# The last two expert loads in 16 transfers of 8 partitions each

## The chip, the cores and the metric

The kernel runs on one core of a Trainium2 chip. The metric is the time of one execution on the device in microseconds (us). TensorE (PE, with its weight loads as PEld), VectorE (DVE), ScalarE (ACT), GpSimd (POOL) and SyncE (SP) run side by side and wait for each other through semaphores. SP computes nothing here: it issues the transfers from the device's memory (HBM) to the on-chip memory of 128 partitions (SBUF). Sixteen DMA engines carry them.

## The reference

Two layers of an encoder on 256 tokens of width 1024, in float32, each sub-layer followed by a residual and a layer norm. Layer 0 mixes by retention and has a dense SwiGLU; layer 1 mixes by stick-breaking attention and has a mixture of experts. The change touches the experts alone:

```python
def moe_swiglu(x, w_router, w_in, w_out):
    ...
    top_val, top_idx = lax.top_k(logits, TOP_K)          # 2 of 8 experts for each token
    ...
    for e in range(N_EXPERTS):
        y = y + gates[:, e:e + 1] * swiglu(xt, w_in[e], w_out[e])
```

Here `swiglu(x, w_in, w_out)` is `(silu(x @ gate) * (x @ up)) @ w_out`, with 3584 hidden columns. The weights of one expert are 7168 x 1024 for `w_in` and 3584 x 1024 for `w_out`, 44 MB in all, and the eight experts' 352 MB are read once.

## The kernel before

The first part (retention, dense channel mixer, attention, router) fills about the first 520 us. In the second, the experts come one after the other, in an order that the router found at run time. SP reads an expert's number from a register, so each of its loads is preceded by an address calculation. Each expert is worked in two units of hidden columns, 2048 and 1536 (`UNITS`). For a unit TensorE multiplies the gathered tokens (in three blocks of 32) with the gate and the up columns (tile `pe`, line 1176), ScalarE and VectorE form `hs` and its transpose `hT`, and TensorE multiplies that with the unit's rows of `w_out` into `po`, also at line 1176.

The weights come in loads of 128 partitions, mostly 1 MB, into tiles called `raw`. A `Stream` keeps the list of them in the order of use. `pump` issues the next one as soon as one of the tiles is free, and a tile is freed (`used`) when its last part has been multiplied. All are issued by SP at line 217, in `chunk`. `by_row_plain` lists the loads of `w_out`: 256 rows each, where partition p takes the rows 2p and 2p + 1, 8 KB that lie together. So the last unit, of 1536 rows, has six; they will be called load 9 to load 14 here, with the eight of the unit before as load 1 to load 8. Each DMA on SP's queue has one of eight semaphores in turn (DMAHW0 to DMAHW7 in the program's rows), and waits, before it is issued, until the DMA that had the same one eight issues earlier has landed.

Behind load 14 SP issues four loads `gbt` of 256 KB (line 1330), the scale and offset of the last layer norm. At the end, TensorE adds up the residual (`psc`, line 1304), multiplies loads 9 to 12 and then loads 13 and 14 into `po`, and runs a few products `warm` (line 434) that nobody reads. `po` is copied to `y` (line 1236), and TensorE returns its rows to their tokens (`psc`, line 1316). The norm's statistics, `ot` (lines 1348 and 1351, then 1370 to 1375) and four stores (line 1366) follow. `by_need` takes the loads in groups of four row blocks at a time from `down`, which is why loads 9 to 12 form one group of eight row blocks and loads 13 and 14 the last.

A second pass of the experts (`more`) is in the program for the case that over 96 tokens choose one expert. It is not run with these inputs.

Of the kernel before, what the change touches and what calls it, by code (L numbers as in the profile page):

```python
# [23 lines left out]
P = 128  # L24
# [16 lines left out]
WARM = (6, 2, 1, 6)  # L41
RAW_MID = 6
RAW_END = 3
HL_BASE = 4
HL_EXTRA = 4

# [137 lines left out]
def trunk_kernel(ctx, tc, x, ret_w_in, ret_w_out, sb_w_kv, sb_w_q, sb_w_out, ln_mix_g, ln_mix_b,  # L184
                 ln_ffn_g, ln_ffn_b, ffn_w_in, ffn_w_out, moe_w_router, moe_w_in, moe_w_out,
                 const_a, const_r, out):
    nc = tc.nc
    ctx.enter_context(tc.manual_schedule())
    consts = ctx.enter_context(tc.tile_pool(name="consts", bufs=1))
    raws = ctx.enter_context(tc.tile_pool(name="raws", bufs=RAW_BASE))  # L190
    hls = ctx.enter_context(tc.tile_pool(name="hls", bufs=HL_BASE))
    res = ctx.enter_context(tc.tile_pool(name="res", bufs=1))
# [5 lines left out]
    def nm(s):  # L198
        cnt[0] += 1
        return f"{s}{cnt[0]}"  # L200
# [3 lines left out]


    def chunk(s, shape, src, cuts, pieces=1, after=None, between=None, plain=False,
              rows="(k p) f -> p k f"):

        def load(slots):
            r = slots.pool.tile([P, CH], F32, tag=slots.tag, name=nm("raw"))[:, :shape[0] * shape[1]]  # L210
            v = r.rearrange("p (k f) -> p k f", k=shape[0])
            for i, c in enumerate(cuts if pieces == 2 else [lambda v: v]):
                if i == 1 and between is not None:
                    between()
                for at, ap in src:
                    ap = ap() if callable(ap) else ap
                    nc.sync.dma_start(c(v[at]), c(ap.rearrange(rows, p=P)))
            if after is not None:
                after()
            return v  # L220
        s.add(load, cuts, plain)

    every = slice(None)

    def by_k(s, parts, after=None, between=None, **kw):

        cuts = [lambda v, i=i: v[:, 2 * i:2 * i + 2, :] for i in range(2)]
        for i in range(2):
            src, o = [], 0
            for ap, c0, n in parts:  # L230
                src.append(((every, every, slice(o, o + n)), ap[i * 512:(i + 1) * 512, c0:c0 + n]))
                o += n
            chunk(s, (4, 512), src, cuts, after=after and (lambda i=i: after(i)),
                  between=between and (lambda i=i: between(i)), **kw)

    def by_block(s, parts, **kw):

        src, o = [], 0
        for ap, c0, n in parts:
            src.append(((every, every, slice(o, o + n)), ap[:, c0:c0 + n]))  # L240
            o += n
        chunk(s, (8, 256), src, [lambda v, i=i: v[:, :, i * P:(i + 1) * P] for i in range(2)], **kw)

    def by_row(s, ap, r0, n, **kw):

        for r in range(r0, r0 + n, 256):
            chunk(s, (2, D), [((every, every, every), ap[r:r + 256, :])],
                  [lambda v, i=i: v[:, i:i + 1, :] for i in range(2)], **kw)

    def by_k_plain(s, ap, c0, n):  # L250

        for k in range(KD):
            chunk(s, (1, n), [((every, every, every), lambda k=k: ap()[k * P:(k + 1) * P, c0:c0 + n])],
                  [lambda v: v[:, 0, :]], plain=True)

    def by_row_plain(s, ap, r0, n):

        for r in range(r0, r0 + n, 256):
            chunk(s, (2, D), [((every, every, every), lambda r=r: ap()[r:r + 256, :])],
                  [lambda v, i=i: v[:, i, :] for i in range(2)], plain=True, rows="(p k) f -> p k f")  # L260

    def split(slots, v):

# [7 lines left out]

    base = Slots(hls, HL_BASE, "w")
    st = Stream([Slots(raws, RAW_BASE)], [base], split)
# [78 lines left out]
    def add_experts(s, which=None):  # L352

        prev = None
        for e in range(NE):
            dyn = e > 0 and which is not None

            def of(w, e=e, dyn=dyn):
                return w[ds(which[e], 1)].rearrange("o a f -> (o a) f") if dyn else w[e]

            for c0, n in UNITS:
                for o in (0, DE):
                    by_k_plain(s, lambda of=of: of(mw_in), o + c0, n)
                if prev is not None:
                    by_row_plain(s, *prev)
                prev = (lambda of=of: of(mw_out), c0, n)
        by_row_plain(s, *prev)

    which = [None] * NE
    add_experts(st, which)  # L370


# [230 lines left out]
    ap = att.enter_context(tc.tile_pool(name="attc", bufs=1, side="right"))  # L603
# [8 lines left out]
    i = (n_ffn - 8) % 8  # L612
# [162 lines left out]
    with tc.tile_pool(name="ffn", bufs=2, side="right") as fp, tc.tile_pool(name="ffn1", bufs=1, side="right") as fp1:  # L775
# [9 lines left out]
        def new_h():  # L785
            return [fp.tile([P, 4, S], FR, tag=tag, name=nm(tag)) for tag in ("hh", "hl")]
# [6 lines left out]
        for j in range(1, 6):  # L793
            old, hs = hs, fp.tile([P, 2, 512], F32, tag="hs", name=nm("hs"))
            if j > 1:
                prev, ht = ht, new_h()
# [12 lines left out]
            if j == 1:  # L809
                for t in range(2):  # L810
                    split_T(old[:, t, :256], *ht, t)
                prev, ht = ht, new_h()
# [56 lines left out]
    with att:  # L869
# [104 lines left out]
        mp2 = ctx.enter_context(tc.tile_pool(name="moe2", bufs=1, side="right", reuse_waits="tile"))  # L974
        raw_end = ctx.enter_context(tc.tile_pool(name="raw_end", bufs=RAW_END, side="right", reuse_waits="tile"))
        st.raws.append(Slots(raw_end, RAW_END))
        st.pump()
# [357 lines left out]
    def more(pos):  # L1335
        st2 = Stream([Slots(raws, RAW_BASE)], [base], split)
        add_experts(st2)
        st2.pump()
        g = one_hot(0, pos)
        experts(st2, pos, gates, g, gather(g), norm)  # L1340
# [62 lines left out]
```

## Time and profile before

| | |
|---|---|
| median of 3 runs | 1369.8 us (1368.88 to 1372.61) |
| the profiled execution | 1371.01 us, span 1369.2 us |
| TensorE busy | 1325.5 us, 97% of the span |
| mean granted TensorE clock | 0.997 |
| read from HBM | 444.08 MB, 325 GB/s over the span |
| DMA rate while the experts run | about 418 GB/s |

[...] Times in the rows count from the first instruction of the span. A busy TensorE is not TensorE at its peak, since matmuls overlap; whether it waits is seen from the idle time in brackets and what ended it. For DMA, the share says how many of the 16 engines are at work, and the time to landing counts from SP's issue to the last arrival.

### The profile page before, as it was taken

Reading aid. Unit: us, or ns where it says so; the run is one execution under the profiler, and the core shown is the slowest. Engines: PE = TensorE matmul, PEld = TensorE weight load, DVE = VectorE, ACT = ScalarE, POOL = GpSimd, SP = SyncE. Lnnn points to the kernel's source line nnn. Section 1 sums busy time; section 2 is a strip of 40 time slices with the busy share of each in tenths; the row PEclk is TensorE's granted clock in tenths of the full one; section 3 lists DMA queues with packets and bytes.
Section 4 is the critical chain, followed back from the end, with each engine's and each line's share of the span. In section 5 each row is a group of like instructions: output and inputs, shape, how many; then the busy total and the mean of one; then the engine's idle time right before and its main releaser. Section 6 shows DMA issues by size and latency. Waiting matters only on the chain. (4 is left out here: it accounts for less than half of the span.)

```text
span 1369.2 us, 30767 instructions
## 1 busy us (share of the span) xinstructions
PE 1325.5 (97%) x13611; PEld 865.6 (63%) x13611; DVE 446.5 (33%) x652; ACT 314.8 (23%) x465; POOL 46.7 (3%) x73
## 2 busy tenths in 40 slices
PE   9999999999999999999989999999999999999986
PEld 7888889999989884354434454563644563554543
DVE  6746667555565554101201200201200200210213
ACT  6544435444437642000100100100100100100101
POOL 0212101000010000000000000000000000000000
PEclk9999999999999999999999999999999999999999
DMA  9865437555649357999999999999999999999993
GB/s 336 295 213 179 160 97 272 179 190 185 185 127 357 131 183 295 393 418 417 418 418 418 416 420 418 417 418 419 400 418 420 406 418 420 401 417 419 405 415 155
DMA packets 122918, 447.40 MB, mean 327 GB/s; under 512 B 9088, under 2 KB 56976, under 8 KB 92048
## 3 DMA queue, kind: packets, MB, share of 16 engines
q1 hardware_dynamic: 121808, 442.01, 82.8%
q0 software_dynamic: 960, 3.15, 0.7%
q8 instruction: 123, 2.02, 0.6%
q14 instruction: 27, 0.22, 0.0%
HBM read 444.08 MB, written 1.05 MB: 325 GB/s over the span
## 5 line engine op out<-in xcount | busy, mean ns | idle before, releaser
L1176 PE MATMUL pe<-raw,xg 128*32 128x384 f32 (+1 forms) x5248 | 506.3, 540 | 13.4 <-PEq L1195 7.4
L1176 PEld LDWEIGHTS pe<-raw,xg 128*32 128x32 f32 x5248 | 203.9, 110 | 305.4 <-issue 266.6
L1176 PE MATMUL po<-raw,hT 128*32 128x256 f32 x4544 | 254.4, 379 | 8.4 <-DMA raw<-in_moe_w_out_dram 5.4
L269 DVE TENSOR_TENSOR w<-raw,w 128x1024 fp32r<-128x1024 f32 x162 | 198.1, 1234 | 144.5 <-ACT w L268 142.2
L1176 PEld LDWEIGHTS po<-raw,hT 128*32 128x32 f32 x4544 | 170.0, 110 | 95.6 <-issue 10.7
L268 ACT CAST w<-raw 128x1024 fp32r<-128x1024 f32 x162 | 168.4, 1048 | 134.6 <-issue 32.1
L1288 DVE TENSOR_TENSOR hs<-hs,pe 128x512 f32<-128x512 f32 (+1 forms) x48 | 29.1, 620 | 362.9 <-PE pe L1176 361.2
L1266 ACT ACTIVATE hs<-pe 128x512 f32<-128x512 f32 (+1 forms) x48 | 25.3, 544 | 457.7 <-PE pe L1176 457.7
L404 PE MATMUL pf<-xT_h,w 128*128 128x256 f32 x448 | 126.9, 283 | 0.0
L406 PE MATMUL pf<-xT_l,w 128*128 128x256 f32 x448 | 126.2, 282 | 0.0
L405 PE MATMUL pf<-xT_h,w 128*128 128x256 f32 x448 | 126.1, 281 | 0.0
L1290 DVE STREAM_TRANSPOSE hT<-hs 128x512 f32<-128x512 f32 (+1 forms) x48 | 27.2, 617 | 237.6 <-PE po L1176 139.2
L404 PEld LDWEIGHTS pf<-xT_h,w 128*128 128x128 f32 x448 | 84.4, 188 | 0.3
L405 PEld LDWEIGHTS pf<-xT_h,w 128*128 128x128 f32 x448 | 84.4, 188 | 0.3
L406 PEld LDWEIGHTS pf<-xT_l,w 128*128 128x128 f32 x448 | 84.4, 188 | 0.0
L1236 ACT COPY y<-po 32x256 f32<-32x256 f32 x48 | 17.5, 364 | 283.3 <-PE po L1176 238.7
L379 PE MATMUL pv<-w,xT_l 128*128 128x512 f32 x96 | 38.4, 400 | 0.0
L381 PE MATMUL pv<-w,xT_h 128*128 128x512 f32 x96 | 38.0, 396 | 0.3 <-DVE w L269 0.3
L380 PE MATMUL pv<-w,xT_h 128*128 128x512 f32 x96 | 37.9, 395 | 0.0
L404 PE MATMUL pq<-xT_h,w 128*128 128x256 f32 x128 | 36.3, 283 | 0.0
L406 PE MATMUL pq<-xT_l,w 128*128 128x256 f32 x128 | 36.0, 281 | 0.0
L405 PE MATMUL pq<-xT_h,w 128*128 128x256 f32 x128 | 36.0, 281 | 0.0
(237 smaller groups left out, 1180.5 us busy)
## 6 DMA issues: line engine op xcount, KB each, us to landing
raw<-in_moe_w_in_dram SPq DMA_DIRECT2D x128, 1024.0 KB, 19.9
raw<-in_moe_w_out_dram SPq DMA_DIRECT2D x112, 1024.0 KB, 19.8
raw<-in_moe_w_in_dram SPq DMA_DIRECT2D x128, 768.0 KB, 15.8
raw<-in_ret_w_in_dram SPq DMA_DIRECT2D x22, 1024.0 KB, 9.3
raw<-in_ffn_w_in_dram SPq DMA_DIRECT2D x20, 1024.0 KB, 5.1
raw<-in_ffn_w_out_dram SPq DMA_DIRECT2D x11, 1024.0 KB, 5.0
raw<-in_ret_w_out_dram SPq DMA_DIRECT2D x8, 1024.0 KB, 5.0
raw<-in_sb_w_kv_dram SPq DMA_DIRECT2D x4, 1024.0 KB, 6.0
```

The lines of the kernel that those rows point to most:

```text
L268: nc.scalar.copy(hv, v)
L269: nc.vector.tensor_sub(lv, v, hv.bitcast(F32))
L379: nc.tensor.matmul(o, sl, mh, start=first, stop=False)
L380: nc.tensor.matmul(o, sh, mh, start=False, stop=False)
L381: nc.tensor.matmul(o, sh, ml, start=False, stop=last)
L404: nc.tensor.matmul(o, lo[:, k, :], xT_h[:, k, :], start=(k == 0), stop=False)
L405: nc.tensor.matmul(o, h[:, k, :], xT_h[:, k, :], start=False, stop=False)
L406: nc.tensor.matmul(o, h[:, k, :], xT_l[:, k, :], start=False, stop=(k == KD - 1))
L1176: nc.tensor.matmul(ov, lhs[r], w, start=first and not (shared and r == 1), stop=last, skip_group_check=True)
L1266: nc.scalar.activation(pairs(hs[:, r, :]), alternate(pg[r]), AF.Silu)
L1288: nc.vector.tensor_mul(pairs(hs[:, r, :]), pairs(hs[:, r, :]), alternate(pu[r]))
L1290: nc.vector.transpose(hT[:, r].rearrange("p k s -> p (k s)"), hs[:, r, :])
```

## The change

`by_row_plain` gets a count of loads, `pieces`, that are cut up. For these, `chunk` issues one DMA for each eight partitions, 16 of 64 KB for one `raw` tile, in place of one DMA of 128 partitions. It is used for the last two loads of the last expert (`LAST8 = 2`): loads 13 and 14, 32 DMAs in place of two. Line numbers behind it grow by four.

```diff
+LAST8 = 2
...
     def chunk(s, shape, src, cuts, pieces=1, after=None, between=None, plain=False,
-              rows="(k p) f -> p k f"):
+              rows="(k p) f -> p k f", parts=(None,)):
...
                     ap = ap() if callable(ap) else ap
-                    nc.sync.dma_start(c(v[at]), c(ap.rearrange(rows, p=P)))
+                    for p0 in parts:
+                        ps = every if p0 is None else slice(p0, p0 + 8)
+                        nc.sync.dma_start(c(v[at])[ps], c(ap.rearrange(rows, p=P))[ps])
...
-    def by_row_plain(s, ap, r0, n):
+    def by_row_plain(s, ap, r0, n, pieces=0):
 
         for r in range(r0, r0 + n, 256):
+            parts = range(0, P, 8) if r >= r0 + n - 256 * pieces else (None,)
             chunk(s, (2, D), [((every, every, every), lambda r=r: ap()[r:r + 256, :])],
-                  [lambda v, i=i: v[:, i, :] for i in range(2)], plain=True, rows="(p k) f -> p k f")
+                  [lambda v, i=i: v[:, i, :] for i in range(2)], plain=True, rows="(p k) f -> p k f", parts=parts)
...
-        by_row_plain(s, *prev)
+        by_row_plain(s, *prev, LAST8)
```

On SP, at the end of the experts, this stood in the program before: load 12 (`raw_11962`), load 13, load 14 and the first of the four `gbt` loads. In brackets are the semaphores that an instruction waits for; PE_49 is TensorE's, for a free tile. An ISA row is an address calculation.

```order
L217 DMA raw_11962<-in_moe_w_out_dram 128x2048 [waits DMAHW2_49,PE_49]
L217 ISA
L217 DMA raw_11977<-in_moe_w_out_dram 128x2048 [waits DMAHW3_49,PE_49]
L217 ISA
L217 DMA raw_11979<-in_moe_w_out_dram 128x2048 [waits DMAHW4_49,PE_49]
L1195 UNCONDITIONAL_BRANCH
L1330 DMA gbt<-in_ln_ffn_g_dram 128x512 [waits DMAHW5_49,PE_49]
```

Now, from load 12 to the ninth transfer of load 13:

```order
L220 DMA raw_11962<-in_moe_w_out_dram 128x2048 [waits DMAHW2_49,PE_49]
L220 ISA
L220 DMA raw_11977<-in_moe_w_out_dram 8x2048 [waits DMAHW3_49,PE_49]
L220 ISA
L220 DMA raw_11977<-in_moe_w_out_dram 8x2048 [waits DMAHW4_49]
...
L220 DMA raw_11977<-in_moe_w_out_dram 8x2048 [waits DMAHW1_49]
L220 ISA
L220 DMA raw_11977<-in_moe_w_out_dram 8x2048 [waits DMAHW2_49]
L220 ISA
L220 DMA raw_11977<-in_moe_w_out_dram 8x2048 [waits DMAHW3_49]
```

The turn of the semaphores goes on through the small transfers: the eighth has that of load 12, the ninth that of the first small one. The `gbt` loads stand behind the last of 32.

On TensorE, the first matmuls of load 13 and load 14, before:

```order
L1176 MATMUL po_12037<-raw_11977,hT_12030 32x256 [waits DMAHW3_49]
L1176 MATMUL po_12037<-raw_11977,hT_12030 32x256 x15
L1176 MATMUL po_12037<-raw_11979,hT_12030 32x256 [waits DMAHW4_49]
L1176 MATMUL po_12037<-raw_11979,hT_12030 32x256 x15
L1195 COMPARE_AND_BRANCH
```

and now, where load 14's tile has got the number 11994:

```order
L1180 MATMUL po_12067<-raw_11977,hT_12060 32x256 [waits DMAHW4_49,DMAHW5_49,DMAHW3_49,DMAHW6_49,DMAHW2_49,DMAHW7_49,DMAHW1_49,DMAHW0_49]
L1180 MATMUL po_12067<-raw_11977,hT_12060 32x256 x15
L1180 MATMUL po_12067<-raw_11994,hT_12060 32x256 [waits DMAHW4_49,DMAHW5_49,DMAHW3_49,DMAHW6_49,DMAHW2_49,DMAHW7_49,DMAHW1_49,DMAHW0_49]
L1180 MATMUL po_12067<-raw_11994,hT_12060 32x256 x15
L1199 COMPARE_AND_BRANCH
```

One semaphore has become eight in each.

## Rows read from the trace of the kernel before

**Rows 1.** The page's slices, 40 of 34 us: DMA busy in tenths, rate.

```profile
DMA  9865437555649357999999999999999999999993
GB/s 336 295 213 179 160 97 272 179 190 185 185 127 357 131 183 295 393 418 417 418 418 418 416 420 418 417 418 419 400 418 420 406 418 420 401 417 419 405 415 155
```

**Rows 2.** Stretches at the end: busy us by engine, granted clock, DMA share, GB/s.

```profile
1310.00:1340.00 30.00, 26.11 (x365) 13.45 (x356) 3.07 (x6) 0.00 (x0) 0.00 (x0) 1.00 1.01 417
1342.00:1349.00 7.00, 6.82 (x129) 3.98 (x125) 0.00 (x0) 0.00 (x0) 0.00 (x0) 1.00 0.46 184
```

**Rows 3.** Order of time at the end, PE, PEld and DVE: start, us, what, idle before.

```profile
1348.13 3.82 PE L1176 MATMUL po<-raw,hT 128*32 128x256 f32 x64 [0.18 <-PEq L1195]
1349.86 1.61 PEld L1176 LDWEIGHTS po<-raw,hT 128*32 128x32 f32 x32 [0.28 <-DMA raw<-in_moe_w_out_dram]
1352.10 1.58 PE L434 MATMUL warm<-ident 128*128 128x128 f32 x12
1354.23 1.10 PE L1316 MATMUL psc<-y,gT 96*128 96x512 f32 x2 [0.56 <-DVE y L1236]
1355.99 2.81 PE L1316 MATMUL psc<-y,gT 96*128 96x512 f32 x6 [0.66 <-DVE y L1236]
...
1360.28 1.41 DVE L1348 SCALAR_TENSOR_TENSOR ot<-psc,mv,gbt 128x512 f32<-128x512 f32 x2 [0.25 <-ACT xa L1318]
```

**Rows 4.** DMA issues, us to landing: at 1307.91; at 1323.51 and 1326.00 alike.

```profile
raw<-in_moe_w_out_dram SPq DMA_DIRECT2D x1, 1024.0 KB, 18.0
...
raw<-in_moe_w_out_dram SPq DMA_DIRECT2D x1, 1024.0 KB, 21.1
```

**Rows 5.** Order of time on SP, some of its issues, duration of the instruction.

```profile
1307.91 0.33 SPq L217 DMA_DIRECT2D raw<-in_moe_w_out_dram  x1
...
1323.51 0.33 SPq L217 DMA_DIRECT2D raw<-in_moe_w_out_dram  x1
1326.00 0.33 SPq L217 DMA_DIRECT2D raw<-in_moe_w_out_dram  x1
1329.80 0.33 SPq L217 DMA_DIRECT2D raw<-in_moe_w_out_dram  x1
```

**Rows 6.** SP's longest wait after 1300: us in total, times, longest.

```profile
SPq L217 <- DMA raw<-in_moe_w_out_dram: 13.0, 6, 3.3
```

**Rows 7.** SP's neighbouring issues in order of time; a wait and `gbr` by line.

```profile
580.99 0.33 SPq L217 DMA_DIRECT2D raw<-in_moe_w_in_dram  x1
581.56 0.33 SPq L217 DMA_DIRECT2D raw<-in_moe_w_in_dram  x1
...
L217 SPq EVENT_SEMAPHORE  x1: 17/17/17, 581.5 to 581.5; - x1
...
L306 SPq DMA_DIRECT2D gbr<-in_ln_mix_g_dram x1: 443/443/443, 43.7 to 43.7; - x1
L306 SPq DMA_DIRECT2D gbr<-in_ln_mix_b_dram x1: 272/272/272, 44.2 to 44.2; - x1
```

**Rows 8.** DMA issues: KB each, us to landing where there is one.

```profile
ident<-in_const_a_dram SPq DMA_DIRECT2D x1, 64.0 KB, 2.0
...
gbr<-in_ln_mix_g_dram SPq DMA_DIRECT2D x1, 4.0 KB
```

**Rows 9.** Stretches in the router stage and at the end; two `pgx` groups, order of time.

```profile
520.50:523.80 3.30, 3.30 (x40) 1.82 (x43) 1.55 (x9) 0.00 (x0) 0.00 (x0) 0.50 1.02 421
524.00:527.00 3.00, 2.98 (x65) 1.71 (x57) 1.77 (x7) 1.50 (x2) 0.00 (x0) 1.00 0.12 45
1358.90:1363.50 4.60, 0.00 (x0) 0.00 (x0) 3.97 (x8) 2.61 (x4) 0.86 (x3) 1.00 0.02 7
1363.60:1369.00 5.40, 0.00 (x0) 0.00 (x0) 2.34 (x4) 0.00 (x0) 0.00 (x0) 0.50 0.52 192
...
520.39 2.79 PE L844 MATMUL pgx<-x,g 128*32 128x256 f32 x24
...
525.48 1.50 PE L844 MATMUL pgx<-x,g 128*32 128x256 f32 x24
```

## The prediction

> **What bounds the kernel now.** I began with the page's slices: from the seventeenth on, the 16 DMA engines are full and move about 418 GB/s, and only the last slice is not full [rows 1]. So the second part, the experts, streams its weights, and the end of the kernel is the end of that stream plus a tail. Then the stretches at the end: 417 GB/s and a DMA share of 1.01 until 1340, but 0.46 between 1342 and 1349 [rows 2]. About half of the engines have run dry by then and the other half is still carrying the last loads. One engine's rate is 417 / 16 = 26 GB/s, so a row of 8 KB takes it 0.31 us.
>
> Next TensorE's last work in order of time [rows 3]. It multiplies the last four row pairs (loads 13 and 14 of the last 3.5 MB unit) from 1348.13 to 1351.95, and its only stop there is 0.28 us, ended by the DMA of load 14. So load 14 lands at about 1349.86, just as TensorE is ready for it. Earlier landings can give at most this 0.28 us; later ones are paid in full, because from there to 1369.2, the span's end, everything hangs on that sum.
>
> Last, SP, which issues the loads. Two rows fit together: the load issued at 1307.91 took 18.0 us to land, that is until 1325.9, and SP's load 13 is issued at 1326.00 [rows 4, 5]. It is the eighth load after that one. The order of the program says the same: each transfer waits for one of eight DMA semaphores in turn, so at most eight transfers are under way. SP waits 13.0 us in six waits for landings of `w_out` after 1300 [rows 6]. Eight transfers of 1 MB cover 8 MB. Eight of 64 KB cover half a megabyte.
>
> **The change part by part.** It removes two issues and adds 32, each with its address calculation. It moves no byte elsewhere and leaves all other engines' work alone, but for the two waits on TensorE: one semaphore becomes eight in each.
>
> *The first eight small transfers* (call them s1 to s8) take the turns that load 13, load 14, the four `gbt` loads and two more had. s1 goes at 1326.00 as load 13 did, s2 at 1329.80 as load 14 did, s3 to s7 each at the landing of one more large load, and s8 at that of load 12, issued at 1323.51: 1323.51 + 21.1 = 1344.6 [rows 4, 5]. That is 0.5 MB in 18.6 us.
>
> *The other 24* can only follow s8. Their own turn is no hindrance: s9 waits for s1, which lies in the queues just behind load 12 and lands at about 1344.9. From there SP's own pace sets the rate. Two neighbouring loads of an expert picked at run time, that waited for nothing long, were issued at 580.99 and 581.56, 0.57 us apart, with an address calculation, a semaphore wait and a move between them [rows 7]. The small ones have one wait where these have two; without the separate wait (17 ns and some 20 around it, an estimate) 0.54 is left. The nearest 8-partition transfers, the two `gbr` loads, took SP 443 and 272 ns where a 128-partition load takes 333, so the bounds are 0.54 - 0.06 = 0.48 and 0.54 + 0.11 = 0.65. I take 0.54, since the 128-partition instruction is the one that was issued in this setting. So s9 goes at 1345.1 and s32 at 1345.1 + 23 x 0.54 = 1357.6 (1356.2 and 1360.1 by the bounds).
>
> *Its landing*: 64 KB took 2.0 us on idle queues at the start [rows 8]. Eight turns of 0.54 are 4.3 us, more than 2.0, so the limit of eight no longer binds. s32 lands at 1359.6 (1358.2 to 1362.1). Before it was 1349.8. **Term 1: +9.8 us** (8.4 to 12.3).
>
> *How the rows are spread*: the only 8-partition transfers, `gbr`, are the only issues without a landing in the list [rows 8]; that view counts sixteen arrivals for a landing, so these two did not run on all 16. [...] If the 64 KB all lay on one engine it would be 8 x 0.31 = 2.5 us per transfer, +50 us over the 24; I give that no weight, since the `gbr` rows were not followed by any slow load.
>
> *TensorE's waits*: eight semaphores in place of one; seven more waits of some 20 to 50 ns, all but the last few passed while s32 is still under way. **Term 2: +0.1 us** (0 to 0.4).
>
> *The clock.* TensorE ends load 12's work at 1348.0, waits for load 13 (s16 at 1348.9, landed by 1350.9), works 1.9 us, and then stands still from 1352.8 to 1359.6, 6.8 us. [...] The price of the lower level stands in the router stage: 24 `pgx` products took 2.79 us there at 0.50 and 1.50 at 1.00, a factor of 1.86 [rows 9]. On load 14's 1.93 us that is +1.7. On all that TensorE does after it (1.93 + 1.58 + 1.10 + 2.81 = 7.4 us) it would be 6.4, less 0.5 that the warm-up products have as slack before `psc`: +5.9. In the router stage, with TensorE at work throughout, the stretch at 0.50 is 3.3 us long and the next is at 1.00 again, so I take the matmuls of load 14 alone. **Term 3: +1.7 us** (0 to 5.9).
>
> *`gbt`*: four loads of 256 KB now follow s32, at 1358.1 to 1359.7, landing by about 1362. Their reader, the first `ot`, ran at 1360.28 in the old trace [rows 3] and moves with everything else to about 1372, so their cover holds with 10 us to spare; without it each microsecond would count.
>
> **Sum**: 9.8 + 0.1 + 1.7 = 11.6 us. The profiled execution took 1371.01 (span 1369.2, and 1.8 around it), so 1382.6 for it. It lies 1.2 above the median of the runs, 1369.8; on that the forecast is 1381.4. No term is a gain; the most that could be won is the 0.28.
>
> **The rivals.**
> 1. *The clock stays or the pace is quicker*: TensorE's pause ends before the clock falls, or SP takes 0.48. 8.4 to 9.8 and no third term: about 1379 (1378 to 1379.7). For it: the new pause of 6.8 us is only 2 longer than the stretch at 1.00 after the last matmul, and at 0.48 it shrinks by 1.4. Against: it is longer all the same. Chance 0.25.
> 2. *Each small transfer is slow, or the clock stays low to the end*: at over 4.3 us from issue to landing the limit of eight sets the pace; at 5 us it would be 0.63 each, +2, and a low clock over the whole tail +4. About 1386. For it: large queues make every landing slow; against: by then the queues are empty. Chance 0.15.
> 3. *The engines, not SP, set the pace*: SP at under 0.31 us per transfer, one row of each on an engine. 1344.9 + 24 x 0.31 = 1352.3, +2.5 on 1369.8, 1372.3, not slower by the bound below. Nothing in rows 7 is that short. Chance 0.03.
> 4. *The other side, not slower*: the half of the engines that ran dry at about 1342 takes the last 2 MB, which then lands earlier, and TensorE loses its 0.28 us stop: 1369.5. It decides if s9 goes out by 1334.9 (24 x 0.54 + 2.0 before 1349.9). For it: the share of 0.46. Against: s8 waits for load 12 until 1344.6, whichever engines s1 takes. Chance 0.04.
> 5. *The change isn't what it says*, the 16 parts being joined again into one: 1369.8. The program has 32 issues, so 0.02.
>
> **How the numbers follow.** The forecast has 0.51: 1381.4, alone from 1379.8 to 1384. The range takes in most of rivals 1 and 2: 1376.5 to 1386. About 0.3%, 4.1 us, is what this measurement can tell from none: slower by more 0.91 (forecast, 1 and 2), within 0.07 (3, 5 and half of 4), faster 0.02 (the other half of 4, for more than the 0.28 us that I can see).
>
> **What would show it.** Right: SP's 24 last small issues about 0.54 us apart from 1345 on; TensorE with a stop of some 2 to 3 us before load 13's products and one of 6 to 7 us before load 14's, both ended by the weights' DMA; the granted clock 0.50 in a stretch around 1357 to 1362; the rest of the tail as before. Wrong: small issues that follow each other long before 1344; a stop of TensorE under 1 us; a time under 1375.

## The result and the profile after

The changed kernel takes 1395.67 us (1392.23 to 1400.57 in four runs), the kernel before 1371.2 on the same chip: the ratio is 1.0177, with a 95% interval of 1.0154 to 1.0200. The change costs 24.5 us; 11.6 were forecast. The profiled execution took 1396.52 us, its span is 1394.7, so 25.5 more than the span before.

First the stretches at the end, with the columns of [rows 2]: us, busy us of PE, PEld, DVE, ACT and POOL, granted clock, DMA share, GB/s.

```profile
1310.00:1340.00 30.00, 26.44 (x391) 13.52 (x384) 2.56 (x6) 0.00 (x0) 0.00 (x0) 1.00 0.97 391
1342.00:1349.00 7.00, 6.45 (x106) 3.28 (x104) 0.00 (x0) 0.00 (x0) 0.00 (x0) 1.00 0.41 151
...
1352.00:1366.00 14.00, 3.64 (x32) 1.57 (x32) 0.00 (x0) 0.00 (x0) 0.00 (x0) 0.60 0.51 73
1354.80:1378.50 23.70, 8.32 (x69) 4.26 (x70) 0.41 (x1) 1.03 (x3) 0.00 (x0) 0.50 0.57 95
1378.70:1383.00 4.30, 3.64 (x14) 1.87 (x14) 3.21 (x7) 1.68 (x4) 0.00 (x0) 1.00 0.01 4
```

Look at share and rate together. In the old stream a DMA share of 1.01 moved 417 GB/s: 417 / (1.01 x 16) = 26 GB/s for each busy engine [rows 2]. Between 1352 and 1366 a share of 0.51 moves 73: that is as much as 8.2 engines busy without a gap, at 8.9 GB/s each. The engines are not waiting for SP here; each of them is slow. This quotient is the reading that decides the case, and it comes back in every experiment. Eight engines also fit the events of the semaphores in the trace: each of s8 to s32 has one update 0.4 to 0.6 us after its issue and eight more up to its landing, where a load of 128 partitions has sixteen updates.

TensorE in order of time, to be held against [rows 3]:

```profile
1349.12 1.93 PE L1180 MATMUL po<-raw,hT 128*32 128x256 f32 x32 [0.67 <-DMA raw<-in_moe_w_out_dram]
1359.18 3.64 PE L1180 MATMUL po<-raw,hT 128*32 128x256 f32 x32 [8.13 <-DMA raw<-in_moe_w_out_dram]
1373.65 3.64 PE L1180 MATMUL po<-raw,hT 128*32 128x256 f32 x32 [10.83 <-DMA gbt<-in_ln_ffn_g_dram]
1377.46 2.13 PE L438 MATMUL warm<-ident 128*128 128x128 f32 x12 [0.17 <-PEq L1199]
1379.60 1.10 PE L1320 MATMUL psc<-y,gT 96*128 96x512 f32 x2
1381.35 2.81 PE L1320 MATMUL psc<-y,gT 96*128 96x512 f32 x6 [0.66 <-DVE y L1240]
```

The three groups at L1180 multiply loads 12, 13 and 14. The one stop of 0.28 us has become two, of 8.13 and 10.83, and loads 13 and 14 take 3.64 us where load 12 takes 1.93. The last stop is put down to `gbt`; the small transfers stand on the same semaphores, and s32 landed at 1373.45. (The views print no landing on a semaphore that also serves transfers with fewer than sixteen updates. Such landings, here and below, are read from the same events.) From there to the end nothing is new: 1.10 and 2.81 for `psc` as before.

SP's issues in order of time (start, time to the end of the last one), and its instructions by kind (ns, least, median, most):

```profile
1326.23 2.83 SPq L220 DMA_DIRECT2D raw<-in_moe_w_out_dram  x2
...
1349.09 4.02 SPq L220 DMA_DIRECT2D raw<-in_moe_w_out_dram  x9
...
1354.58 11.86 SPq L220 DMA_DIRECT2D raw<-in_moe_w_out_dram  x14
...
L220 SPq DMA_DIRECT2D raw<-in_moe_w_out_dram x25: 276/277/278, 1349.1 to 1366.2; - x25
L220 SPq FUSED_REGOPS  x24: 46/46/51, 1349.4 to 1365.5; - x24
...
SPq L220 <- DMA raw<-in_moe_w_out_dram: 33.0, 26, 3.0
```

The row at 1349.09 is s8 to s16, (4.02 - 0.28) / 8 = 0.468 us apart: SP's own pace. The row at 1354.58 is s19 to s32, (11.86 - 0.28) / 13 = 0.891 apart, though the instruction still takes 277 ns. The last row is the wait for landings after 1300: 26 waits and 33.0 us, where it was 6 and 13.0 [rows 6]. SP is held by its turns: each transfer waits until the eighth before it has landed, and a landing now takes 7.1 us, which is 8 x 0.89.

Some 2.7 us of the 25.5 do not come from the change. In the router stage this execution spent 13.4 us at the lower clock, where the one before spent 3.3 [rows 9]:

```profile
518.60:532.00 13.40, 13.40 (x123) 7.13 (x127) 6.15 (x28) 2.84 (x4) 0.00 (x0) 0.50 0.40 166
```

From 600 us on SP issues its loads 2.0 to 2.8 us later than before, most of them 2.6, and load 12 2.7. The profile of e7_one_load shows this long stretch too, that of e5_by_16 the short one, so it is not tied to the small transfers.

### The profile page after: what moved, and what is told of

Read it like the earlier page. It is cut to its first block, busy times and chain, and to the rows that moved or that the text cites. A ratio compares the mean times of both kernels' runs of the same rounds, so it can differ in the third digit from the quotient of the medians.

```text
span 1394.7 us, 30865 instructions
## 1 busy us (share of the span) xinstructions
PE 1334.7 (96%) x13611; PEld 870.1 (62%) x13611; DVE 446.7 (32%) x652; ACT 314.6 (23%) x465; POOL 46.7 (3%) x73
## 5 line engine op out<-in xcount | busy, mean ns | idle before, releaser
L1180 PE MATMUL pe<-raw,xg 128*32 128x384 f32 (+1 forms) x5248 | 507.8, 540 | 13.2 <-PEq L1199 6.6
L1180 PEld LDWEIGHTS pe<-raw,xg 128*32 128x32 f32 x5248 | 203.9, 110 | 306.7 <-issue 263.8
L1180 PE MATMUL po<-raw,hT 128*32 128x256 f32 x4544 | 257.2, 383 | 26.7 <-DMA raw<-in_moe_w_out_dram 12.9
L1180 PEld LDWEIGHTS po<-raw,hT 128*32 128x32 f32 x4544 | 172.2, 111 | 114.1 <-issue 31.3
```

What stands on the lines that cost most here:

```text
L1180: nc.tensor.matmul(ov, lhs[r], w, start=first and not (shared and r == 1), stop=last, skip_group_check=True)
```

## Experiments

Every kernel is the changed one with one more edit. "Load 14 after load 12" is the time from the landing of load 12 to that of load 14: 5.2 us before, 24.4 in the changed kernel. "GB/s per busy engine" is the quotient above, from one row of the stretches in each kernel.

### Which side of the transfer is slow

*e1_both_far, e2_source_far, e3_dest_far* take, for the eight rows of each small transfer, partitions four apart inside a block of 32, or the rows in HBM that belong to these: both sides, the source alone, the destination alone. In e2 and e3 rows of `w_out` come to other partitions than they should, so their output is not the reference's.

```diff
-  ps = every if p0 is None else slice(p0, p0 + 8)
+  near = every if p0 is None else slice(p0, p0 + 8)
+  far = every if p0 is None else slice(p0 // 32 * 32 + p0 % 32 // 8, p0 // 32 * 32 + 32, 4)
-  nc.sync.dma_start(c(v[at])[ps], c(ap.rearrange(rows, p=P))[ps])
+  nc.sync.dma_start(c(v[at])[far], c(ap.rearrange(rows, p=P))[far])     # e1; e2: [near], [far]; e3: [far], [near]
```

Expected of e1_both_far:

> As the changed kernel, 32 transfers of 8 partitions, but the eight partitions lie four apart (0, 4, ... 28, and so on), and with them the eight rows in HBM. In the changed kernel a transfer took 0.88 us of its engines where 0.31 was expected. Theory 'destination' (eight neighbouring partitions are slow to write) and theory 'source' (64 KB that lie together in HBM are slow to read): the packets fall back to about 0.31 us, SP's pace of 0.47 sets the rate, load 14 lands 13 us after load 12 in place of 24, and the time is about 1381. Theory 'small transfers' (an engine with one row per transfer is slow whatever the place): 0.88 stays, about 1395.

Of e2_source_far:

> As the changed kernel with neighbouring partitions, but the eight rows that each transfer reads lie four rows apart in HBM (rows of w_out go to other partitions than they should, so the result is not the reference's; the bytes and the work are the same). Theory 'destination': 0.88 us per transfer stays, about 1395. Theory 'source': about 0.31 us per packet, time about 1381. Theory 'small transfers': 1395.

Of e3_dest_far:

> As the changed kernel, reading 64 KB that lie together, but writing eight partitions that lie four apart (rows go to other partitions than they should, same bytes and work). Theory 'destination': about 0.31 us per packet, time about 1381. Theory 'source': 0.88 stays, about 1395. Theory 'small transfers': 1395.

Measured: 1390.49 us (ratio 1.0126, 1.0087 to 1.0166), 1395.0 (1.0159, 1.0123 to 1.0195) and 1392.64 (1.0144, 1.0101 to 1.0187). SP's small issues by kind and a stretch, first of e1, then of e2, then of e3:

```profile
L221 SPq DMA_DIRECT2D raw<-in_moe_w_out_dram x24: 627/644/692, 1345.4 to 1365.3; - x24
...
1350.00:1364.00 14.00, 3.64 (x32) 1.61 (x32) 0.00 (x0) 0.00 (x0) 0.00 (x0) 0.60 0.25 76
```

```profile
L221 SPq DMA_DIRECT2D raw<-in_moe_w_out_dram x13: 276/277/278, 1352.4 to 1363.5; - x13
...
1353.00:1363.00 10.00, 3.29 (x32) 1.58 (x32) 0.00 (x0) 0.00 (x0) 0.00 (x0) 0.67 0.52 72
```

```profile
L221 SPq DMA_DIRECT2D raw<-in_moe_w_out_dram x23: 627/645/693, 1347.5 to 1366.5; - x23
...
1350.00:1364.00 14.00, 3.22 (x32) 1.55 (x32) 0.00 (x0) 0.00 (x0) 0.00 (x0) 0.65 0.25 76
```

With a far source nothing changes: 72 / (0.52 x 16) = 8.7 GB/s per busy engine, landings at 7.2 us. With a far destination it is 19, and landings come after 2.2 to 2.5 us. But the time of about 1381 that the destination theory promised did not come: SP's instruction takes 645 ns for stepped partitions, not 277, so SP issues every 0.845 us and load 14 comes 23 us after load 12 all the same. One cost was taken away and another of the same size put in its place. I first took this for proof that the destination is the cause; it isn't yet, since at 0.845 us these kernels ask for 77 GB/s only, hardly more than the slow ones get.

*e10_every_2nd and e11_every_16th* have the same weakness: both sides take every second partition of 16, or every sixteenth of 128.

```diff
-  ps = every if p0 is None else slice(p0, p0 + 8)
+  ps = every if p0 is None else slice(p0 // 16 * 16 + p0 % 16 // 8, p0 // 16 * 16 + 16, 2)   # e11: slice(p0 // 8, P, 16)
```

Expected of e10_every_2nd and e11_every_16th:

> Each small transfer takes every second partition of sixteen, on both sides. Theory A (rows that go to neighbouring partitions share a way in): half as many rows share one, so a row takes 0.44 us and not 0.88, landings fall from 7 us to 2 or 3. SP's instruction: if any step between partitions makes it dearer, 645 ns, as with a step of four, SP's pace 0.85 and the time again about 1391; if its price grows with the distance, less than 645, and the time lies between 1382 and 1391. Rival (sixteen partitions are as near as eight): rows stay at 0.88 and landings at 7 us, about 1395.

> Each small transfer takes every sixteenth partition of all 128, on both sides. Theory A with neighbours alone: no two rows share a way in, rows as in the kernels with a step of four (0.31 to 0.55 us), landings 2.3 us, SP's instruction 645 ns, about 1391. Rival (the ways in are shared in another pattern than by neighbours, so that partitions 16 apart meet): rows at 0.44 or more, landings longer than 2.4 us.

Measured: 1391.44 and 1392.52 us in one run each, SP's instruction 644 and 584 ns (median), 20.7 and 18.8 GB/s per busy engine. So a step of two costs SP as much as a step of four, and a step of sixteen somewhat less, where 645 was expected. On the destination they say no more than e1.

*f1_fixed_near, f2_fixed_far and f4_fixed_far_two* ask for more. The small transfers read expert 1's rows, at an address that is known beforehand, which spares SP the address calculation (the output is not the reference's); f1 keeps neighbouring partitions, f2 takes those four apart, and f4 lets ScalarE's queue issue every second one of them.

```diff
-  [((every, every, every), lambda r=r: ap()[r:r + 256, :])],
+  [((every, every, every), lambda r=r, fixed=len(parts) > 1: (mw_out[1] if fixed else ap())[r:r + 256, :])],
...
-  nc.sync.dma_start(c(v[at])[ps], c(ap.rearrange(rows, p=P))[ps])          # ps as in e1 for f2 and f4
+  (nc.scalar if p0 and p0 % 16 else nc.sync).dma_start(c(v[at])[ps], c(ap.rearrange(rows, p=P))[ps])   # f4
```

Expected of f1_fixed_near, f2_fixed_far and f4_fixed_far_two:

> The changed kernel, but its 32 small transfers read expert 1's rows, an address known beforehand, and not those of the expert that the routing chose (the output is not the reference's): SP needs no address calculation, so it can issue every 0.3 to 0.4 us. Both theories: rows of 0.88 us, transfers 0.88 apart once eight are under way, load 14 lands about 24 us after load 12, time about 1394.

> The same fixed rows, with partitions four apart on both sides. SP's instruction stays at 645 ns, without the address calculation the pace is 0.65 to 0.72, so 91 to 100 GB/s are asked for. Theory A (the way into neighbouring partitions carries 74 GB/s, partitions four apart have more): no queue, rows 0.31 to 0.55, landings at 2.3 us, load 14 lands 18 to 20 us after load 12, time about 1386. Theory Q (rows slow down when transfers overlap, wherever they go): landings grow to 7 us, transfers 0.88 apart, about 1394.

> As f2_fixed_far, but every second small transfer is issued by ScalarE's queue, so that two sequencers ask together for up to 180 GB/s. Theory A: rows 0.31 to 0.55 us, transfers follow each other at 0.35 to 0.45 us, 145 to 190 GB/s, which eight neighbouring partitions never took. Theory Q: rows of 0.88 us or more, 74 GB/s again. The time itself depends on what ScalarE's work does behind its issues, and decides nothing.

Measured in one run each: 1393.51, 1389.15 and 1383.34 us. SP's issues and a stretch of f1:

```profile
1348.43 13.92 SPq L220 DMA_DIRECT2D raw<-in_moe_w_out_dram  x16
...
1349.00:1356.00 7.00, 1.03 (x12) 0.66 (x16) 0.00 (x0) 0.00 (x0) 0.00 (x0) 0.71 0.54 75
```

of f2:

```profile
1347.39 16.73 SPq L220 DMA_DIRECT2D raw<-in_moe_w_out_dram  x25
...
1349.00:1356.00 7.00, 2.36 (x44) 1.22 (x36) 0.00 (x0) 0.00 (x0) 0.00 (x0) 0.78 0.31 94
```

and of f4:

```profile
1349.00:1356.00 7.00, 3.09 (x44) 1.51 (x36) 0.00 (x0) 0.00 (x0) 0.00 (x0) 0.74 0.42 133
```

f1 could issue every 0.34 us and is held to (13.92 - 0.27) / 15 = 0.91: 75 GB/s, 8.7 per busy engine. f2 issues every (16.73 - 0.62) / 24 = 0.67 us without ever being held, lands after 2.3 to 2.6 us, and moves 94 GB/s at 19 per busy engine; f4 moves 133 at 20. It had been expected to move 145 to 190 and is held by its turns, with landings after 3.2 to 4.7 us. One transfer lands every 0.49 us there, so seven to eight are under way, about as many as in the changed kernel. So eight rows to partitions four apart were written at nearly twice the rate at which eight neighbours took them (133 against 75 GB/s), with as many transfers overlapping. Both sides are far in f2 and f4, but e2 has cleared the source. The destination is shown to be the cause, and the rival (rows slow down when transfers overlap, wherever they go) has fallen. In f2 load 14 came 18.6 us after load 12, as expected (18 to 20); its time lay 3 us above what I named.

### What the limit goes by

*e5_by_16, e6_by_32, e8_by_4_one, g2_fixed_by_4* change the number of partitions: 16, 32, and twice 4 (e8 only in load 14, the address calculated; g2 in both loads, from fixed addresses).

```diff
-  ps = every if p0 is None else slice(p0, p0 + 8)
+  ps = every if p0 is None else slice(p0, p0 + 16)      # e6: 32; e8, g2: 4
-  parts = range(0, P, 8) if r >= r0 + n - 256 * pieces else (None,)
+  parts = range(0, P, 16) if r >= r0 + n - 256 * pieces else (None,)
```

Expected of e5_by_16, e6_by_32, e8_by_4_one and g2_fixed_by_4, in this order:

> The last two loads in transfers of 16 neighbouring partitions: 16 of 128 KB in place of 32 of 64 KB. The runs so far: neighbouring partitions of the destination made a transfer of 8 rows take 0.88 us, wherever the rows lie in HBM. Theory 'shared way in' (about four neighbouring partitions have one way into SBUF, which carries some 37 GB/s, so 16 rows take as long as 8): again 0.88 us per transfer; eight transfers are left after load 12, so load 14 lands about 2 + 8 x 0.88 = 9 us after load 12 (5.2 before the change, 24.4 with it), +4 to +6 with the clock, about 1376. Theory 'per byte of a transfer' (a small transfer moves at 74 GB/s however many partitions): 1.76 us each, 16 us after load 12, about 1385. If 16 engines get full speed: 0.47 each, 5.8 after load 12, about 1372.

> The last two loads in transfers of 32 neighbouring partitions, eight of 256 KB in all, so all of them go out in the eight turns by the time load 12 lands. Theory 'turns' with 'shared way in': the eighth goes at load 12's landing and lands 3 us later, earlier than load 14 did before (5.2); TensorE has no stop left, time that of the kernel before within 2 us. Theory 'per byte of a transfer': 3.5 us each, the last three in a queue, load 14 lands 6 to 10 us after load 12, +1 to +6.

> Only load 14, in 32 transfers of 4 neighbouring partitions (32 KB each). Theory 'shared way in': four rows still take 0.88 us, 24 transfers are left after load 13, load 14 lands 2.5 + 2 + 24 x 0.88 = 26 us after load 12, about 1393 to 1396. If the time goes with the bytes (0.44 us for four rows), SP's 0.47 sets the pace: 2.5 + 2 + 11.3 = 16 us after load 12, 1383 or so.

> Both loads in transfers of 4 neighbouring partitions with rows of 8 KB, 64 in all, from fixed addresses, at 0.30 to 0.34 us, so 96 to 109 GB/s are asked for. If the limit lies with the bytes into a group of neighbours: a queue, 0.44 us per 32 KB, landings of 3.5 us or more, about 1395. If four rows at a time are never short, where eight are: 0.31 to 0.34 apart, landings of 2 to 2.5 us, about 1388.

Measured: 1381.42 us (ratio 1.0067, 1.0038 to 1.0096), 1380.56 (1.0058, 1.0040 to 1.0077), 1383.81 (1.0083, 1.0057 to 1.0109), and 1392.57 in one run. A stretch of e5, then SP's issues and a stretch of e8, then a stretch of g2:

```profile
1347.00:1355.00 8.00, 2.35 (x40) 1.13 (x32) 0.00 (x0) 0.00 (x0) 0.00 (x0) 1.00 1.01 146
```

```profile
L220 SPq DMA_DIRECT2D raw<-in_moe_w_out_dram x26: 252/253/254, 1347.3 to 1361.0; - x26
...
1351.00:1361.00 10.00, 0.88 (x18) 0.26 (x8) 0.00 (x0) 0.00 (x0) 0.00 (x0) 0.67 0.22 67
```

```profile
1349.00:1356.00 7.00, 0.00 (x0) 0.00 (x0) 0.00 (x0) 0.00 (x0) 0.00 (x0) 0.63 0.22 75
```

Sixteen neighbours keep all 16 engines busy (1.01) at 146 GB/s, 9.0 per engine: twice the neighbours, twice the rate, a row still as slow, 0.9 us per 128 KB. Load 14 came 11.3 us after load 12 (9 expected), and the time is 5 us above the 1376 named. The 32-partition kernel missed its expectation in another place: load 14 came 7.3 us after load 12 (3 expected), and load 12 itself took 25.2 us to land, where it was 21.1 [rows 4].

Four neighbours surprised me. e8 asked for a transfer every 0.44 us, got it, and its engines ran at 19 GB/s: the theory that groups of four share one way of half the eight's rate said 0.88 and has fallen. g2 asked for 96 to 109 GB/s and got 75, again with SP held back; but its share is 0.22, so 3.5 engines at 21 GB/s each: hardly fewer than a transfer has rows, and each at more than twice the 8.9 of the changed kernel.

*e9_half_rows, f3_fixed_half, g1_fixed_4kb* halve the rows to 4 KB. In e9 and f3 one half of the columns goes as one transfer of 128 partitions and only the other half in eights (f3 from fixed addresses); in g1 each eight is sent as two transfers of 4 KB rows, 64 in all, from fixed addresses.

```diff
-  nc.sync.dma_start(c(v[at])[ps], c(ap.rearrange(rows, p=P))[ps])
+  if p0 == 0:                                                    # e9, f3
+      nc.sync.dma_start(c(v[at])[:, 0, :], c(ap.rearrange(rows, p=P))[:, 0, :])
+  nc.sync.dma_start(c(v[at])[p0:p0 + 8, 1, :], c(ap.rearrange(rows, p=P))[p0:p0 + 8, 1, :])   # g1: k = 0 and 1
```

Expected of e9_half_rows, f3_fixed_half and g1_fixed_4kb:

> Of each of the two loads one half of the columns goes as one transfer of 128 partitions (512 KB), and only the other half as 16 transfers of 8 neighbouring partitions, whose rows are then 4 KB. Theory A (the way into eight neighbouring partitions carries some 74 GB/s): a transfer is served in 0.44 us, just under SP's pace of 0.47, so SP sets the pace again, landings stay at 2 to 3.5 us, load 14 lands 14 to 17 us after load 12, and the time is about 1382, as the prediction had it. Theory B (each small transfer costs 0.88 us whatever its bytes): 0.88 apart from the tenth on, latency 7, load 14 lands 23 to 26 us after load 12, about 1394.

> Of the two fixed loads one half of the columns as one transfer of 128 partitions, the other half as 16 of 8 neighbouring partitions with rows of 4 KB; SP at 0.3 to 0.4 us, so 80 to 107 GB/s are asked for. Theory A: the queue comes back, 0.44 us for 32 KB, rows of 4 KB at 0.44 and not 0.175 in the end, landings of 2.5 to 3.5 us; load 14 lands 13 to 15 us after load 12. Theory Q (the number under way decides): either rows stay at 0.175 and SP sets the pace, or they go to 0.88. Time 1378 to 1381 by A.

> Both loads whole in transfers of 8 neighbouring partitions, but each partition's 8 KB as two transfers of 4 KB, 64 in all, from fixed addresses (expert 1), at SP's pace of 0.34 us, so 96 GB/s are asked for over 20 us. Theory A (the way into eight neighbours carries 74 GB/s, and f3_fixed_half was too short to show it): after some 5 us rows of 4 KB go to 0.44 us, landings to 3.5 us, transfers 0.44 apart, load 14 lands about 26 us after load 12, about 1395. Theory R (rows of 8 KB are slow, rows of 4 KB not): 0.34 apart throughout, landings of 2 us, load 14 lands 19 to 21 us after load 12, about 1388.

Measured: 1380.0 us (ratio 1.0046, 1.0029 to 1.0063), and 1378.03 and 1394.68 in one run each. SP's issues of e9, then of f3 with a stretch, then of g1 with a stretch:

```profile
1353.30 7.69 SPq L224 DMA_DIRECT2D raw<-in_moe_w_out_dram  x16
```

```profile
1348.07 6.41 SPq L224 DMA_DIRECT2D raw<-in_moe_w_out_dram  x16
...
1351.00:1356.00 5.00, 1.07 (x16) 0.42 (x16) 0.00 (x0) 0.00 (x0) 0.00 (x0) 0.96 0.31 90
```

```profile
1344.78 24.78 SPq L223 DMA_DIRECT2D raw<-in_moe_w_out_dram  x52
...
1349.00:1356.00 7.00, 0.00 (x0) 0.00 (x0) 0.00 (x0) 0.00 (x0) 0.00 (x0) 0.50 0.53 69
```

e9 is the prediction's own picture of the transfers: SP issues every (7.69 - 0.28) / 15 = 0.49 us, the service is quicker than that, nothing queues, and load 14 lands 15.4 us after load 12, where the prediction had 15.0. So SP's pace would have set the sum if the service had been as quick as assumed. The loss is smaller than forecast, 0.46% or some 6 us of the 11.6; half of each load comes whole here, and TensorE has less left to do at the end. f3 asked for 96 GB/s and showed no queue in the 6.4 us of its last sixteen eights, against theory A. g1 asked for the same over 20 us and was held to (24.78 - 0.27) / 51 = 0.48 us per 32 KB, 69 GB/s, 8.1 per busy engine, with landings at 4 us: half the bytes, about half the time. So the 8 KB row as such isn't the cause.

But bytes per second don't decide it alone, and f3 wasn't too short to show a queue. At the same pace of 0.34 us nine of its small transfers in a row land after 1.9 to 2.1 us each, while the first nine of g1 behind load 12 take 1.9, 2.2, 2.6, 2.6, 2.9, 2.9, 3.2, 3.2 and 3.4. (In the changed kernel the rows of s8 took 0.40 us, those of the fourth transfer from there on 0.88.) What differs is that g1 sends two transfers in a row to the same eight partitions, and f3 goes on to the next eight each time. That this is the reason is not shown; no run tests it.

### The turns alone, and the amount

*e4_columns* keeps 16 transfers of 64 KB per load, but each has all 128 partitions and 128 columns. *e7_one_load* splits load 14 alone.

```diff
-  nc.sync.dma_start(c(v[at])[ps], c(ap.rearrange(rows, p=P))[ps])      # e4
+  k, f = p0 // 64, slice(p0 % 64 * 16, p0 % 64 * 16 + 128)
+  nc.sync.dma_start(c(v[at])[:, k, f], c(ap.rearrange(rows, p=P))[:, k, f])
...
-LAST8 = 2                                                             # e7
+LAST8 = 1
```

Expected of e4_columns and e7_one_load:

> The last two loads again as 16 transfers of 64 KB each, but each of all 128 partitions and 128 columns (512 B per partition), so that every transfer is spread over all engines and partitions. It keeps the number of transfers and the turns of eight semaphores. Theory 'turns' (s1 to s8 wait for the large loads, the other 24 follow at SP's pace): load 14 lands about 12 us after load 12, TensorE stops once for 6 to 8 us, +9 to +12 on the kernel before, about 1381. If the count of transfers cost nothing and all came from where the rows lie: within 2 us of before, about 1371. If small transfers are slow as such: 1395.

> Only load 14 in 16 transfers of 8 partitions, load 13 whole. Theory 'turns' with 'shared way in': the eighth small transfer waits for load 13 (2.5 us after load 12), eight more follow at 0.88 each, load 14 lands 2.5 + 2 + 7 = 11.5 us after load 12, so +6.3 and some of the clock: 1378 to 1381. If the loss grew with the bytes in small transfers alone: half of the full change's, 1383 or so.

Measured: 1380.73 us (ratio 1.0069, 1.0045 to 1.0092) and 1386.1 (1.0101, 1.0060 to 1.0141). The issues of e4 with their landing:

```profile
raw<-in_moe_w_out_dram SPq DMA_DIRECT2D x24, 64.0 KB, 1.9
```

Here a 64 KB transfer lands 1.9 us after its issue, about as `ident` did [rows 8], SP's pace is 0.525 us, and so the limit of eight doesn't bind (8 x 0.525 is 4.2). Two of SP's issues took 1.4 and 1.6 us, and load 14 came 17.3 us after load 12, not the 12 expected. The loss is 0.69%, some 9 us, not far from the 11.6 forecast for the change. So the turns and SP's pace cost about 9 us by themselves, and the eight neighbours add about 15 to that. (TensorE works on columns there as they come, with nine waits of 5.2 us in all, so the two kernels are not alike in all else, and the split of the loss is an estimate.) In e7, load 14 came 13.6 us after load 12, and the small ones landed 0.84 to 1.19 us apart behind load 13, the slowest while the `gbt` loads ran beside them. The theory of the turns had 11.5 us and 1378 to 1381, and both were exceeded. It is about half the loss for half the split.

### The clock

In e5_by_16 the same 32 matmuls stand on both sides of a fall of the clock. Load 13's and load 14's groups there, in order of time, and the stretches that hold them:

```profile
1350.35 1.93 PE L1180 MATMUL po<-raw,hT 128*32 128x256 f32 x32 [2.93 <-DMA raw<-in_moe_w_out_dram]
1356.92 3.64 PE L1180 MATMUL po<-raw,hT 128*32 128x256 f32 x32 [4.63 <-DMA gbt<-in_ln_ffn_g_dram]
```

```profile
1350.30:1352.30 2.00, 1.93 (x32) 1.13 (x32) 0.00 (x0) 0.00 (x0) 0.00 (x0) 1.00 1.11 156
1356.90:1360.60 3.70, 3.64 (x32) 1.56 (x32) 0.00 (x0) 0.00 (x0) 0.00 (x0) 0.50 0.27 96
```

At a granted clock of 1.00 they take 1.93 us, at 0.50 3.64. That is the third term, 1.7 us. The pause alone doesn't say which it will be: in e6_by_32 load 14's group ran in 1.93 after a pause of 1.75, but the two groups before it, after pauses of 2.18 and 0.49, took 2.52 and 2.70, partly at 0.50.

## Why the prediction was wrong

The direction, the place and most of the mechanism were right; the size was half. Against the forecast's own terms:

- *s1 to s8* went as described: s8 was issued at 1349.09, as load 12 landed (1349.07). That is 4.5 us later than the 1344.6 foreseen: load 12 went out 2.7 later, as all loads since the router stage, and took 22.8 us to land, not 21.1. I had charged the small transfers with no effect on the large ones. Half a megabyte of slow rows in the same queues may explain the 1.7 us. For it: load 12 took 22.7 to 23.4 us with eight neighbours in both loads (e2, f1), 25.2 in e6, and 20.5 to 21.3 with a destination four apart (e1, e3, f2, f4). Against it: 22.1 and 22.7 with steps of two and sixteen (e10, e11). So it stays open.
- *SP's pace*: 0.468 us for 0.54. My bounds were 0.48 and 0.65: the 8-partition instruction is cheaper (277 ns) than the one I chose (333), so the pace lies at, even just below, the lower bound. It hardly mattered, because from s19 on SP's pace no longer set the rate.
- *The step that failed* is "From there SP's own pace sets the rate", and with it "Eight turns of 0.54 are 4.3 us, more than 2.0, so the limit of eight no longer binds". Both need a small transfer to be served in less than 0.54 us. One row on an engine at 0.31 us would do; that was my estimate, and no row of the kernel before shows how eight rows are spread or what they cost. The spread was as good as that (8.2 engines at work, eight updates for eight rows). But an 8 KB row took 0.88 us, since all eight went to neighbouring partitions (f1 at 8.7 GB/s per busy engine, f2 at 19). The rate of an engine was read from 128-partition loads [rows 2], and a landing of 2.0 us from one transfer on idle queues [rows 8]; neither shows what a row of eight neighbours in a full queue costs. With 0.89 the eighth transfer before has not landed when SP is ready, the limit of eight binds, and from load 12's landing to s32's it takes 24.4 us, not 15.0.
- *Term 1* is therefore 20.9 us in place of 9.8: 9.8, and 9.4 for the slow rows, and 1.7 for load 12. *Term 2* is right: TensorE's first weight load of load 14 starts 0.17 us after s32's landing, where it started 0.04 after that of load 14 before, so 0.1. *Term 3* is right to a tenth: 3.64 - 1.93 = 1.7. It needs the clock to fall while TensorE stands still: the granted clock is 0.50 from 1354.8 on, 3.7 us after load 12's products, where [rows 9] have a first stretch of 4.6 us at 1.00 behind TensorE's last work; and it is back at 1.00 for `psc`, as assumed. With the 2.7 of the router stage, that is the 25.5 of the span to within 0.1.
- *Rival 2* was the true case by its first half: the limit of eight set the pace. I gave it a landing of 5 us and 0.63 us each, 1386; it was 7.1 and 0.89. The argument held against it, that the queues are empty by then, was true of the large loads and beside the point: the small transfers make a queue of their own.

What stays open: why eight neighbours are slow (four get 75 GB/s in g2, from 3.5 busy engines at 21 each; eight get the same 75 in f1, from 8.6 at 8.7); why f3 shows no queue where g1 does; and load 12's later landing. No experiment beat the kernel before, whose stop there was only 0.28 us.

## What to carry to other kernels

The limit of eight under way counts transfers here, not bytes: with the last loads split, eight of them covered half a megabyte in place of eight megabytes. The time then became their number times the issuer's pace (0.49 us in e9) or the service of one (0.89 us in the changed kernel), whichever was longer. That service has to be read from a transfer with the same destination in a queue, not from wide loads or a lone one. And when an experiment takes a cost away and the time hardly moves, look whether another of the same size has come in, as SP's 645 ns did here.

## What was not expected of the hardware

- In small transfers that followed each other closely, rows of 8 KB to eight or sixteen neighbouring partitions went at 8.7 to 9.0 GB/s per busy engine (changed kernel, e2, f1, e5); to partitions two, four or sixteen apart, or to four neighbours, at 19 to 21 (e1, e3, f2, f4, e10, e11, e8, g2); in loads of 128 partitions at 26 [rows 2].
- With a calculated address SP's DMA instruction took 253 ns for four neighbouring partitions (e8), 277 for eight (changed kernel), 315 for sixteen (e5), 333 for 128 (e4), and 644 to 645 for eight with a step of two or four between them (e10, e1), 584 with a step of sixteen (e11). A step of four on the destination's side alone made it 645 (e3), one on the source's side alone left it at 277 (e2).
